# Queries and keys of a hybrid attention layer by Strassen's scheme: a projection stage of its own, operands through DRAM

## The chip, the cores and the metric

The kernel runs on one core of a Trainium2 chip. The metric is the device time of one execution in microseconds, here the median of three runs. TensorE (PE in the profile) multiplies matrices, VectorE (DVE) and ScalarE (ACT) work elementwise, GpSimd (POOL) does some elementwise work and issues DMAs that the other queues cannot, and SyncE (SP) issues most of the DMAs.

## The reference

One decoder layer over a sequence of 1024 tokens of width 1024, in float32:

```python
h = rms_norm(x, pre_mix_g)
qa, ka, va, qb, kb, vb, gates = split(h @ w_in)       # 512 x3, 1536 x3, 2048 columns
qa, ka = rope(qa), rope(ka)                           # 4 heads x 2 parts of 64
oa = diff_attention(qa, ka, va, lam)                  # causal, softmax1 - lam * softmax2
ya = rms_norm(oa) * (1 - lam_init) @ w_a_out
qb, kb = rope(qb), rope(kb)                           # 3 groups x 4 heads of 128
outs, lses = dilated_group(...)                       # windows 128, 512, 2048; dilations 1, 4, 16
yb = (softmax(lses) weighted sum of outs) @ w_b_out
x = x + rms_norm((sigmoid(g_a) * ya + sigmoid(g_b) * yb) @ w_mix_out)
u = causal_depthwise_conv(rms_norm(x) @ w_up)         # 2 x 2816 channels
x = x + rms_norm((gelu(u_gate) * u_val) @ w_down)
```

## The kernel before

Every float32 operand is split into a high and a low part (`split`: ScalarE writes the rounded high part, VectorE the remainder), and every product is three matmuls, high x high, low x high and high x low (`mm3`, L155 to L157). x is held transposed as `xh` and `xl`, the eight chunks of 128 channels side by side; the norm's factor is applied after the product (`rstd_row`, and inside the rope tables).

The program runs in stages. The *value stage* computes the 2048 value columns by Strassen's scheme in Winograd's form: x is cut into quarters (b11, b12, b21, b22), three sums of them (t2, t3, t4) stand beside the quarters, and a fourth (minus t1) stands in b12's own place; seven products of half the depth take the place of eight. Afterwards b12 is loaded again and split (`again`, `split_x`). Values go to DRAM (`v_d`) in POOL's queue, and so do the rope tables (`tab_d`).

Then come *queries, keys, gates and attention*. `proj_t` computes one block of 128 columns: two halves of 512 tokens, eight chunks, 48 matmuls. For a query or key `rotated` applies the rope (L684 to L687: ScalarE swaps the halves, VectorE multiplies and adds), and the high and low parts are written straight into `slot` tiles (18 of them, 512 KB each, used by operands and values alike). For a gate `put_gate` scales the block and stores it to `gt_d`.

Attention is a row of jobs. In attention A (four heads) a job is a block of 128 queries: `attend_a` computes both scores, a masked reduction on VectorE (L770), the exponential on ScalarE (L777), and the two softmaxes' combination (L784). Transposes on TensorE (L697), their split, and the products with the values (L710, L713) are put off by `later` to following jobs. In attention B there are twelve steps (two pairs of heads x three groups x two heads) of four jobs (`attend_b`: scores L155 to L157 into `s`, reduction L975, exponential L981, output L1009). Outputs and their statistics go to DRAM and are merged over the three groups by `merge`, whose loads are in POOL's queue.

`interleave` weaves the pieces of projections between the jobs by weight: in A, the query and key of the next head and the gates named in `A_FILLS` ("g" a gate, "p" the next head, "P" the first step of B, "v", "w", "x", "V" values); in a step of B, the query and key of the next step; in the last step three gates (`B_GATES`). The order of the instructions on each engine comes from a planner that runs the program against a cost model, with priorities where `high_priority` raises them; the chip then runs each engine's list in order. `issue_after` (`behind_marks`) holds some work behind marked instructions.

After attention come the two output projections (`branch`), the mixing product, the up projection with its convolution (the first blocks plain, the other nineteen by the same scheme of seven products, `seven`), the down projection by seven products, and the norms.

Of the kernel before, what the change touches and what calls it, by code (L numbers as in the profile page):

```python
# [15 lines left out]
F32 = mybir.dt.float32  # L16
# [33 lines left out]
START_GATES, A_FILLS, B_GATES = 1, ("gpgg", "gpvgg", "wgpgg", "xgPVgg"), 3  # L50
# [37 lines left out]
def trunk(ctx: ExitStack, tc: tile.TileContext, a, out):  # L88
# [133 lines left out]
    c_d = dram.tile([NF, P, S], F32, name="c_d")  # L222

# [90 lines left out]
    rstd_row = open_pool(attn, "row", side="right").tile([P, S], F32, name="rstd_row")  # L314
    st_a = ExitStack()
# [5 lines left out]
    tb = open_pool(st_v, "tb", side="right")  # L321
# [12 lines left out]

    def new_tabs():
        return [tabs.tile([P, S], F32, tag=t, name=t) for t in ("cos", "sin")]
# [17 lines left out]
    def load_tabs(first, n):  # L354

        cos, sin = new_tabs()
        for q in range(P // n):
            to = slice(q * n, (q + 1) * n)
            dma(cos[to], tab_d[0][first : first + n])
            dma(sin[to], tab_d[1 if q % 2 else 2][first : first + n])  # L360
        return cos, sin

# [11 lines left out]
    def sums_x(k, low, high):  # L374
# [3 lines left out]
        e, o = (tb.tile([P, 2, 512], F32, tag=t, name=t) for t in ("sin", "cos"))  # L378
# [17 lines left out]
    def norm_x(m):  # L396
# [5 lines left out]
        if m < 8:  # L402
            rows_x.append(tb.tile([P, S], F32, tag=("kk", "ang", "sin", "cos")[m % 4], name="rows"))
            nc.gpsimd.dma_start(rows_x[m], a["x"][m * P : (m + 1) * P])
# [40 lines left out]
    with ExitStack() as st_y:  # L445
# [17 lines left out]
        def more_tags():  # L463

            for tag in itertools.cycle(("ang", "kk", "sin", "cos")):
                t = tb.tile([P, S], F32, tag=tag, name="raw")
                for sl in halves():
                    yield t[:, sl]
                    yield next(rt_tags)
# [142 lines left out]
        made, fetched, again = 12, 14, []  # L612
# [3 lines left out]
        for n in range(8, len(steps_v)):  # L616
# [15 lines left out]
            if n == ANGLES_AT:  # L632
                pos = [load_raw(a["positions"][sl].partition_broadcast(P), next(tags)) for sl in halves()]
                args = [tb.tile([P, S], F32, tag=n_, name=n_) for n_ in ("sin", "cos")]
# [20 lines left out]
    tabs = open_pool(attn, "tabs", side="right")  # L655
    cos_a, sin_a = load_tabs(64, 32)
# [21 lines left out]

    def rotated(ps, cos, sin, sl, quarter):
        t1 = rt.tile([P, 512], F32, tag="t1", name="t1")  # L680
        t2 = rt.tile([P, 512], F32, tag="t2", name="t2")
        for q in range(P // quarter):
            src, dst = slice((q ^ 1) * quarter, ((q ^ 1) + 1) * quarter), slice(q * quarter, (q + 1) * quarter)
            nc.scalar.activation(t1[dst], ps[src], AF.Copy)  # L684
        nc.vector.tensor_tensor(t2, ps, cos[:, sl], op=ALU.mult)  # L685
        nc.vector.tensor_tensor(t1, t1, sin[:, sl], op=ALU.mult)
        nc.vector.tensor_tensor(t2, t2, t1, op=ALU.add)  # L687
        return t2
# [37 lines left out]
    def proj_a(h, res):  # L726
        q0, q1, k0, k1, l0, l1 = (slot(n) for n in ("q0", "q1", "k0", "k1", "l0", "l1"))
        res += [q0, q1, k0, k1, l0, l1]

        def put_q(half, sl, ps):  # L730
            t = rotated(ps, cos_a, sin_a, sl, 32)
            nc.scalar.activation(q0[u, sl], t[u], AF.Copy)
            nc.scalar.activation(q1[v, sl], t[v], AF.Copy)
            nc.vector.tensor_tensor(q0[v, sl], t[u], q0[u, sl].bitcast(F32), op=ALU.subtract)
            nc.vector.tensor_tensor(q1[u, sl], t[v], q1[v, sl].bitcast(F32), op=ALU.subtract)

        def put_k(half, sl, ps):
            t = rotated(ps, cos_a, sin_a, sl, 32)
            for part, kk in ((u, k0), (v, k1)):
# [1003 lines left out]
```

## Time and profile before

| | |
|---|---|
| Median of three runs | 1696.95 us (1696.14 to 1698.37) |
| The profiled execution | 1697.3 us, its span 1695.3 us |
| Granted TensorE clock | 0.998 |
| TensorE / VectorE / ScalarE / GpSimd busy | 1682.1 / 1333.5 / 891.8 / 106.3 us |
| DMA | 216.41 MB, 128 GB/s over the span |

A group's row gives source line, engine, operation, tiles and shape, count, then busy us and mean ns of one, then the engine's idle time before such instructions and what ended it. A row of the view by stretches gives the stretch in us from the start, its length, the busy us of PE, PEld (weight loads), DVE, ACT and POOL with the number of instructions, the granted clock, the share of time that the DMA engines were busy, and GB/s. A row of the chain gives start, length, engine, line and count of the work that ended last. In a row of a DMA stand the tile and its source, the queue, the count, the size and the median us to landing. The tile `acc` is the PSUM bank that projections write; `s`, `pt` and `o` are those of attention. Line numbers are those of the kernel before.

### The profile page before, as it was taken

To read this page: it belongs to the slowest core of one execution; us is meant where nothing else is said; L and a number is where in the kernel's file an instruction comes from. 1 tells how busy PE (TensorE), PEld (TensorE's weight loads), DVE (VectorE), ACT (ScalarE), POOL (GpSimd) and SP (SyncE) were. 2 spreads that over 40 slices of the span, in tenths; PEclk is the share of its full clock that TensorE was granted. 3 is DMA by queue.
4 is the path that set the end of the run, shared out by engine and by line. 5 is a ranking of instruction groups with operands and counts; after the bars stand their busy time and mean duration, and the time that the engine had idled before them with its cause. 6 is when DMAs were issued, how large, how long until landed. Compare 5 with 4: busy or idle time off the path is not lost.

```text
span 1695.3 us, 22960 instructions
## 1 busy us (share of the span) xinstructions
PE 1682.1 (99%) x8078; PEld 1410.0 (83%) x8078; DVE 1333.5 (79%) x2445; ACT 891.8 (53%) x1663; POOL 106.3 (6%) x174
## 2 busy tenths in 40 slices
PE   9999999999999999999999999999999999999997
PEld 7888888888888888888888888888888888888886
DVE  8795686877776766677756865899999989799967
ACT  7643575656454776666653533464444445355453
POOL 0031000000000000000123400300000000000000
PEclk9999999999999999999999999999999999999999
DMA  8677311214112213233585631132222222296524
GB/s 266 234 253 235 99 60 62 86 59 119 50 63 81 70 53 108 86 112 119 200 285 186 203 118 63 38 106 92 95 81 75 98 83 88 95 343 214 193 75 161
DMA packets 104451, 216.41 MB, mean 128 GB/s; under 512 B 12992, under 2 KB 22144, under 8 KB 104336
## 3 DMA queue, kind: packets, MB, share of 16 engines
q1 hardware_dynamic: 89296, 171.28, 30.5%
q0 software_dynamic: 10288, 35.28, 6.1%
q10 hardware_dynamic: 4752, 8.39, 1.3%
q8 instruction: 63, 1.03, 0.3%
q14 instruction: 52, 0.43, 0.1%
HBM read 167.05 MB, written 47.86 MB: 127 GB/s over the span
## 4 chain that ended last, share of the span: by engine, by line
PE 97%; DMA 2%; DVE 1%; ACT 1%; issue 0%; SPq 0%; DVEq 0%
PE acc L155 22%; PE acc L156 22%; PE acc L157 22%; PE acc L1578 3%; PE acc L1579 3%; PE acc L1577 3%; PE o L710 2%; PE pt L697 2%; PE acc L1258 2%; PE acc L1256 2%; PE acc L1257 2%; PE o L713 1%; PE s L156 1%; PE s L157 1%; PE s L155 1%; PE s L768 1%
## 5 line engine op out<-in xcount | busy, mean ns | idle before, releaser
L156 PE MATMUL acc<-xh,wlo 128*128 128x512 f32 x768 | 303.2, 395 | 0.0
L157 PE MATMUL acc<-xl,whi 128*128 128x512 f32 x768 | 303.1, 395 | 0.0
L155 PE MATMUL acc<-xh,whi 128*128 128x512 f32 x768 | 303.0, 395 | 0.0
L149 ACT ACTIVATE whi<-raw 128x512 fp32r<-128x512 f32 (+1 forms) x252 | 156.1, 626 | 170.3 <-PE acc L157 88.1
L146 DVE TENSOR_TENSOR wlo<-raw,whi 128x512 fp32r<-128x512 f32 (+1 forms) x252 | 178.8, 717 | 40.4 <-ACT whi L149 34.7
L156 PEld LDWEIGHTS acc<-xh,wlo 128*128 128x128 f32 x768 | 144.4, 188 | 27.8
L157 PEld LDWEIGHTS acc<-xl,whi 128*128 128x128 f32 x768 | 144.5, 188 | 27.5
L155 PEld LDWEIGHTS acc<-xh,whi 128*128 128x128 f32 x768 | 144.4, 188 | 27.3
L155 PE MATMUL acc<-mh,whi 128*128 128x512 f32 x400 | 155.8, 390 | 0.3 <-ACT mh L149 0.3
L156 PE MATMUL acc<-mh,wlo 128*128 128x512 f32 x400 | 155.6, 389 | 0.0
L157 PE MATMUL acc<-ml,whi 128*128 128x512 f32 x400 | 155.3, 389 | 0.0
L684 ACT ACTIVATE t<-acc 64x512 f32<-64x512 f32 (+1 forms) x160 | 94.7, 592 | 55.3 <-PE acc L157 53.3
L1454 DVE TENSOR_TENSOR u<-acc,u 128x512 f32<-128x512 f32 x133 | 91.3, 691 | 20.3 <-PE acc L157 20.1
L149 ACT ACTIVATE whi<-s 128x512 fp32r<-128x512 f32 x76 | 46.9, 627 | 102.3 <-PE acc L157 88.1
L685 DVE TENSOR_TENSOR t<-acc,cos 128x512 f32<-128x512 f32 x64 | 44.1, 690 | 67.1 <-ACT t L684 63.5
L155 PEld LDWEIGHTS acc<-mh,whi 128*128 128x128 f32 x400 | 75.1, 188 | 16.0 <-ACT mh L149 0.5
L156 PEld LDWEIGHTS acc<-mh,wlo 128*128 128x128 f32 x400 | 75.1, 188 | 15.6
L157 PEld LDWEIGHTS acc<-ml,whi 128*128 128x128 f32 x400 | 75.1, 188 | 15.5
L1578 PE MATMUL acc<-whi,wlo 128*128 128x512 f32 x220 | 77.6, 390 | 0.0
L1577 PE MATMUL acc<-whi 128*128 128x512 f32 x220 | 76.4, 389 | 0.0
L1579 PE MATMUL acc<-wlo,whi 128*128 128x512 f32 x220 | 73.2, 390 | 0.0
L777 ACT ACTIVATE s<-s,mx 128x896 f32<-128x896 f32 (+7 forms) x64 | 49.4, 772 | 36.9 <-DVE mx L770 21.0
(387 smaller groups left out, 3941.6 us busy)
## 6 DMA issues: line engine op xcount, KB each, us to landing
raw<-in_w_in SPq DMA_DIRECT2D x96, 256.0 KB, 2.9
raw<-in_w_up SPq DMA_DIRECT2D x88, 256.0 KB, 2.8
raw<-in_w_v SPq DMA_DIRECT2D x71, 256.0 KB, 4.7
raw<-c_d SPq DMA_DIRECT2D x48, 256.0 KB, 3.8
c_d<-c SPq DMA_DIRECT2D x22, 512.0 KB, 2.7
raw<-in_w_down SPq DMA_DIRECT2D x37, 256.0 KB, 4.1
v_d<-yv POOLq DMA_DIRECT2D x32, 256.0 KB, 4.5
gt_d<-gate ACTq DMA_DIRECT2D x32, 256.0 KB, 2.1
```

Source lines behind the costliest of these rows:

```text
L146: eng.tensor_tensor(lo, src, hi.bitcast(F32), op=ALU.subtract)
L149: copy = nc.scalar.activation(hi, src, AF.Copy)
L155: nc.tensor.matmul(o, sh, mh, start=first, stop=False, skip_group_check=on)
L156: nc.tensor.matmul(o, sl, mh, start=False, stop=False, skip_group_check=on)
L157: nc.tensor.matmul(o, sh, ml, start=False, stop=last, skip_group_check=on)
L684: nc.scalar.activation(t1[dst], ps[src], AF.Copy)
L685: nc.vector.tensor_tensor(t2, ps, cos[:, sl], op=ALU.mult)
L777: exp = nc.scalar.activation(sc[c][:, :w], sc[c][:, :w], AF.Exp, bias=mx[:, c, 0:1], scale=-1.0, accum_out=den[:, c : c + 1])
L1454: nc.vector.tensor_tensor(to, made(p), x, op=ALU.add)
L1577: nc.tensor.matmul(banks[m], gh[:, tk], wh, start=f == 0, stop=False)
L1578: nc.tensor.matmul(banks[m], gl[:, tk], wh, start=False, stop=False)
L1579: nc.tensor.matmul(banks[m], gh[:, tk], wl, start=False, stop=f == NH - 1)
```

## The change

A stage of its own, behind the value stage, computes all sixteen query/key pairs by seven products: query and key block of a head are the two halves of the columns, and the quarters and sums of x from the value stage are used once more. The four sums of the weight quarters (s1 to s4) are made in a tile that ScalarE or a load fills first, and to which DMAs of POOL's queue add the rest. ScalarE and VectorE evacuate, rotate and split each pair over 1024 tokens, and four stores put it into `qk_d`, already in the order that the dilation needs. xh is restored after this stage instead of inside the value stage. Attention loads its operands: twelve loads of 256 KB for a head of A, four of 512 KB for a step of B. What is woven between the jobs is now gates alone, in pieces of six matmuls (a gate is eight pieces): one gate at the start, 20, 20, 16 and 16 pieces in the heads of A, four in each of eleven steps of B, and four in the last.

```diff
-START_GATES, A_FILLS, B_GATES = 1, ("gpgg", "gpvgg", "wgpgg", "xgPVgg"), 3
+START_GATES, A_FILLS, B_GATES = 8, ("gpgggg", "gpgvggg", "wgpggg", "xgPgVgg"), 4
...
+    qk_d = dram.tile([2 * (AH + BG * BH), 2, P, S], F32, name="qk_d")
...
-            if (p, i) == ("p5", 1):
-
-                again.append(load_raw(a["xT"][k][:, 512:], next(tags)))
-            if (p, i) == ("p6", 1):
-                with behind_marks():
-                    split_x(k, halves()[1], again[k])
+    with ExitStack() as st_q:
+        pq = open_pool(st_q, "pq")
+        ops_q = dict(p1=("a11", b11), p6=("s2", t2), p2=("a12", b21), p7=("s3", t3), p5=("s1", b12), p4=("a22", t4), p3=("s4", b22))
+        slots_q = itertools.cycle([slot_w, slot_w, lambda: slot_w(pq, 3)])
...
+        def weights_q(n):
...
+            def start_sum(name, src, scale=None):
+                t = pq.tile([P, 512], F32, tag="s", name=name, bufs=4)
+                if scale:
+                    nc.scalar.activation(t, src, AF.Copy, scale=scale)
+                else:
+                    dma(t, src)
+                return t
+
+            def add_to(t, src):
+                nc.gpsimd.dma_start(t, src, accum_op=ALU.add)
+
+            a11 = load_raw(d11, next(tags))
+            s1 = start_sum("s1", d21)
+            put_w("a11", a11)
+            s3 = start_sum("s3", s1, -1.0)
+            add_to(s1, d22)
+            add_to(s3, d11)
+            s2 = start_sum("s2", a11, -1.0)
+            add_to(s2, s1)
+            a12 = load_raw(d12, next(tags))
+            a22 = load_raw(d22, next(tags))
+            put_w("s2", s2)
+            put_w("a12", a12)
+            s4 = start_sum("s4", s2, -1.0)
+            add_to(s4, d12)
+            put_w("s3", s3)
+            put_w("s1", s1)
+            put_w("a22", a22)
+            put_w("s4", s4)
...
+        def rotate_q(n, c, u, tab):
...
+            for q in range(P // quarter):
+                src, dst = slice((q ^ 1) * quarter, ((q ^ 1) + 1) * quarter), slice(q * quarter, (q + 1) * quarter)
+                nc.scalar.activation(sw[dst], u[src], AF.Copy)
+            nc.vector.tensor_tensor(u, u, tab[0], op=ALU.mult)
+            nc.vector.tensor_tensor(sw, sw, tab[1], op=ALU.mult)
+            nc.vector.tensor_tensor(u, u, sw, op=ALU.add)
...
+                split(*(t.rearrange("p (r i) -> p r i", r=dil) for t in (hi, lo)), u.rearrange("p (i r) -> p r i", r=dil))
+            for i, t in enumerate((hi, lo)):
+                dma(qk_d[2 * head + c, i], f32(t))
+
+        def seven_q(n, ws, tab):
...
+            left = next(banks_q)()
+            made("p1", left, True)
+            with tc.high_priority(offset=60):
+                nc.scalar.activation(c11, left, AF.Copy)
+            down = next(banks_q)()
+            made("p6", down, True)
+            plus_q(c12, down, c11)
+            made("p2", left)
+            made("p7", down)
+            plus_q(c22, down, c11)
+            right = next(banks_q)()
+            made("p5", right, True)
+            plus_q(c22, right, c22)
+            made("p4", down)
+            plus_q(c21, down, c11)
+            with tc.high_priority(offset=60):
+                nc.scalar.activation(c11, left, AF.Copy)
+            made("p3", right)
+            plus_q(c12, right, c12)
+            for c, u in enumerate(us):
+                rotate_q(n, c, u, tab)
...
+        for n in range(len(pairs)):
+            following = weights_q(n + 1) if n + 1 < len(pairs) else None
+            if n == AH:
+                tab = load_tabs(0, 64)
+            seven_q(n, ws, tab)
+            ws = following
+        again = [load_raw(a["xT"][k][:, 512:], next(tags)) for k in range(4)]
+        with tc.high_priority(offset=60):
+            for k in range(4):
+                split_x(k, halves()[1], again[k])
...
-    def proj_a(h, res):
+    def load_a(h, res):
...
+        for to, src in ((q0[u], qh[u]), (q0[v], ql[u]), (k0[u], kh[u]), (k0[v], kh[u]), (l0[u], kl[u]), (l0[v], kl[u]),
+                        (q1[v], qh[v]), (q1[u], ql[v]), (k1[u], kh[v]), (k1[v], kh[v]), (l1[u], kl[v]), (l1[v], kl[v])):
+            dma(f32(to), src)
...
-    def proj_b(g, h, res, between=None):
+    def load_b(g, h, res):
+        ops = [slot(n) for n in ("qh", "ql", "kh", "kl")]
+        res += ops
+        at = order.index(QB + g * 512 + h * P)
+        for n, t in enumerate(ops):
+            dma(f32(t), qk_d[at + n // 2, n % 2])
...
-        fill = proj_b(nxt[1], nxt[2], ops_b[nxt], functools.partial(split_b, *nxt[:2]) if h % 2 else None)
-        interleave(jobs(todo), 4, (itertools.chain(fill, once(load_ots)) if nxt == steps[-1] else fill, 8))
+        fills = [(once(functools.partial(load_b, *nxt[1:], ops_b[nxt])), 0), gates(2)]
+        if h % 2:
+            fills.append((once(functools.partial(split_b, *nxt[:2])), 0))
+        fills.append(gates(2))
+        if nxt == steps[-1]:
+            fills.append((once(load_ots), 0))
+        interleave(jobs(todo), 4, *fills)
```

More of the change, by code (lines that the diff above doesn't have):

```diff
@@ L852, in head_norm @@
         later(3, norm)
-    free_gates = list(range(2 * KC))
+    supply = itertools.chain(*(gate(i) for i in range(2 * KC)))
     def gates(n):
-        todo = [free_gates.pop(0) for _ in range(n)]
-        return itertools.chain(*(gate(i) for i in todo)), 4 * n
+        return itertools.islice(supply, n), n * 0.5
     def run(gen):
```

121 lines of the change are left out of this document (56 added, 65 removed).

## The prediction

> **What bounds the kernel now.** I read the page's busy line and chain first, then the busy time by stage, then the chain restricted to one stage, which gives true matmul intervals.
>
> ```profile
> span 1695.3 us, 22960 instructions
> PE 1682.1 (99%) x8078; PEld 1410.0 (83%) x8078; DVE 1333.5 (79%) x2445; ACT 891.8 (53%) x1663; POOL 106.3 (6%) x174
> PE 97%; DMA 2%; DVE 1%; ACT 1%; issue 0%; SPq 0%; DVEq 0%
> ...
> L155 PE MATMUL acc<-xh,whi 128*128 128x512 f32 x768 | 303.0, 395 | 0.0
> ```
> ```profile
> 26.00:162.00 136.00, 136.00 (x603) 112.42 (x604) 111.55 (x196) 69.49 (x120) 23.07 (x40) 1.00 0.71 235
> 162.00:865.00 703.00, 703.00 (x3743) 601.25 (x3742) 497.21 (x1180) 430.68 (x901) 24.67 (x44) 1.00 0.30 97
> 240.00:545.00 305.00, 305.00 (x1616) 261.01 (x1614) 225.27 (x588) 166.04 (x350) 1.14 (x4) 1.00 0.23 76
> 545.00:865.00 320.00, 320.00 (x1781) 275.53 (x1780) 221.06 (x501) 216.43 (x472) 21.06 (x34) 1.00 0.35 117
> 1110.00:1480.00 370.00, 370.00 (x1633) 306.28 (x1632) 338.01 (x452) 161.24 (x222) 3.79 (x39) 1.00 0.26 89
> ```
>
> The second view lists stretch, length, then busy us of PE, PEld, DVE, ACT, POOL, then clock, DMA share, GB/s. Its rows are the value projection (26 to 162), all queries, keys, gates and attention (162 to 865), inside it attention A (240 to 545) and B (545 to 865), and the up projection by Strassen's scheme (1110 to 1480). TensorE has no gap in any of them. The kernel is bound by the number of matmuls, so only that number, or a new gap, can move the time.
>
> The 395 ns of a matmul is not its price: matmuls overlap. 1633 of them in 370 us are 0.2266 us each, and the chain agrees with four in 0.91 us:
>
> ```profile
> 1505.28 0.91 PE acc L1577 x4
> ```
>
> **The change, part by part.**
>
> *Fewer matmuls.* A query/key pair is 2 columns x 2 halves x 8 chunks x 3 = 96 matmuls; with seven products of 4 chunks it is 84. Sixteen pairs save 192 x 0.2266 = 43.5 us. By the 395 ns of the group row it would look like 76 us, which is why I take the interval. The profiled execution took 1697.3 us (span 1695.3 and 2.0 around it; the median of the runs is 1696.95, 0.35 lower), so without a single new gap the kernel would take 1697.3 - 43.5 = 1653.8 us. Everything else is a question of new gaps.
>
> *The query/key stage (16 x 84 x 0.2266 = 19.04 us each pair).* Its costs on the other engines, by these rows:
>
> ```profile
> L146 DVE TENSOR_TENSOR wlo<-raw,whi 128x512 fp32r<-128x512 f32 x40 | 27.5, 688 | 5.4 <-ACT whi L149 5.2
> L1454 DVE TENSOR_TENSOR u<-acc,u 128x512 f32<-128x512 f32 x133 | 91.3, 691 | 20.3 <-PE acc L157 20.1
> L1339 DVE SCALAR_TENSOR_TENSOR c<-u,cw,c 128x1024 f32<-128x1024 f32 x44 | 55.2, 1284 | 3.9 <-ACT c L1338 3.4
> L1343 DVE TENSOR_TENSOR c<-c 128x1024 f32<-128x1024 f32 x22 | 26.9, 1224 | 0.1
> 572.52 2.12 DVE L878 TENSOR_TENSOR kl<-t,kh 128x512 fp32r<-128x512 f32 x2 [0.33 <-ACT kh L877]
> L149 ACT ACTIVATE whi<-raw 128x512 fp32r<-128x512 f32 x40 | 25.2, 629 | 17.2 <-PE acc L157 16.7
> L684 ACT ACTIVATE t<-acc 32x512 f32<-32x512 f32 x32 | 18.9, 590 | 7.6 <-PE acc L157 7.2
> L149 ACT ACTIVATE vh<-vperm 128x1024 fp32r<-128x1024 f32 x16 | 16.5, 1048 | 0.1
> ```
>
> DVE: 7 weight remainders and 5 additions to PSUM at 0.69, 6 wide rotations and 2 remainders at 1.22, together 18.1 us. In the 8 pairs with a dilation of 4 or 8 the remainders read strided, 2.12 each, and it is 19.9. The up projection is my scale: there a block also has 84 matmuls, and 17 operations at 0.69, 4 at 1.28 and one at 1.22 sum to 18.1, while the row shows 338/370 x 19.04 = 17.4 busy and no gap. By that ratio the strided pairs need 19.1, as much as TensorE. ACT: 7 splits and 3 scaled copies at 0.63, 2 copies from PSUM at 0.59, 2 splits at 1.05, and 8 part copies in an attention A pair (the A row shows that 32 partitions cost what 64 do; over 1024 columns 1.05), 18.1 us; in a B pair only 4 such copies. Every evacuation has one product, 12 x 0.2266 = 2.72 us, before TensorE needs its bank again, and one strided remainder can stand in front of it. I take 0.5 us in each of 8 strided pairs: +4 us (0 to 16, all sixteen at 1 us).
>
> *The accumulating DMAs* are not in this trace. Nearest rows:
>
> ```profile
> raw<-in_w_in SPq DMA_DIRECT2D x96, 256.0 KB, 2.9
> v_d<-yv POOLq DMA_DIRECT2D x32, 256.0 KB, 4.5
> og<-og_d POOLq DMA_DIRECT2D x8, 768.0 KB, 6.4
> ```
>
> Each is 256 KB from POOL's queue: 4.5 us if it is a plain transfer, 9 if reading and writing the target doubles it. A set of weights has three in series (s1, s2, s4) behind one load: 2.9 + 3 x 4.5 + copies, about 19 us, or 32. Weights are issued a pair ahead, and nine operand slots serve seven products, so up to 1.7 pairs (32 us) cover it; I take nothing. Uncovered, ACT's copy s4 = -s2 stands in its queue waiting for the DMA, the copies of c11 behind it, and product p2 behind those: that is the second rival. Bytes are no bound here: 8 x 0.26 + 4 x 0.52 = 4.2 MB per 19.04 us is 220 GB/s, below the 235 of the value stage. Against a gain: POOL's queue is otherwise empty then.
>
> *Into and out of the stage.* The first pair's sums wait for buffers of the value stage while its stores run on POOL: +1 us. The restore of xh (four 256 KB loads, four splits) moves from the value stage, past the last pair's stores in SP's queue; the first gate's second half needs it 5.4 us into START_GATES; +2 (0 to 6).
>
> *Attention A.* Four heads lose 8 units of projection and get 80 pieces of gates in all (a piece is 6 matmuls, 1.36 us), 20 or 16 a head. From the chain:
>
> ```profile
> by line: PE acc L156 24.0%; PE acc L155 23.9%; PE acc L157 23.9%; PE o L710 6.0%; PE s L768 5.1%; PE pt L697 5.1%; PE s L767 5.0%; PE o L713 3.4%; PE o L839 2.1%; PE pt L847 1.1%; PE s L155 0.2%; PE s L156 0.2%; PE s L157 0.2%
> L156 PE MATMUL acc<-xh,wlo 128*128 128x512 f32 x343 | 136.2, 397 | 0.0
> L155 PE MATMUL acc<-xh,whi 128*128 128x512 f32 x342 | 135.8, 397 | 0.0
> L157 PE MATMUL acc<-xl,whi 128*128 128x512 f32 x342 | 135.8, 397 | 0.0
> ```
>
> The first row (240 to 540) gives 28% of 300 us to attention, some 21 us a head. With 27 or 22 us of gates a head falls from 76 to 49 or 44 us. DVE had 225 us in 305, 56 a head. At 0.69 an operation it loses 40 (24 of rotating and splitting a q and a k column, 4 of their weights, 12 of three gates; 27.6 us) and gets 10 for 2.5 gates (6.9): 35 of 49 us. It does not become the bound, but there is less to run while the softmax goes round: +3 (0 to 10).
>
> ```profile
> POOL mask_b L938 <- DMA oa_d<-osb: 353.8, 1, 353.8
> ```
>
> B's first reduction needs mask_b, and POOL makes it only behind A's last store. The end of A (weight 12 of the last head's 64) has 3 pieces, 4 us, of gates beside it instead of 10: +2 (0 to 6).
>
> *Attention B.* The last three rows are of 545 to 865: 1027 projection matmuls, 232.7 us, leave 87.3 for attention. With 48 pieces (65.3 us) the stage needs 152.6 us of TensorE, 12.7 a step instead of 26.7. ACT had 216 us; the rows below take 44.5, 21.1, 19.0 and 23.9 from it, and 12 splits for gates put 7.5 back: 115, no bound. DVE (221) loses as much. The transfers are the new thing:
>
> ```profile
> L684 ACT ACTIVATE t<-acc 64x512 f32<-64x512 f32 x75 | 44.5, 593 | 22.7 <-PE acc L157 21.7
> L877 ACT ACTIVATE kh<-t 128x512 fp32r<-128x512 f32 x20 | 21.1, 1058 | 14.9 <-DVE t L687 14.9
> L877 ACT ACTIVATE qh<-t 128x512 fp32r<-128x512 f32 x18 | 19.0, 1057 | 10.5 <-DVE t L687 10.5
> L149 ACT ACTIVATE whi<-raw 128x512 fp32r<-128x512 f32 x38 | 23.9, 628 | 2.8 <-PE acc L157 2.3
> ```
> ```profile
> DMA packets 18410, 37.40 MB, mean 117 GB/s; under 512 B 2941, under 2 KB 7197, under 8 KB 18385
> raw<-in_w_in SPq DMA_DIRECT2D x36, 256.0 KB, 2.8
> gt_d<-gate ACTq DMA_DIRECT2D x5, 256.0 KB, 3.8
> GB/s 266 234 253 235 99 60 62 86 59 119 50 63 81 70 53 108 86 112 119 200 285 186 203 118 63 38 106 92 95 81 75 98 83 88 95 343 214 193 75 161
> 860.00:870.00 10.00, 10.00 (x51) 8.45 (x50) 3.26 (x6) 5.47 (x7) 0.53 (x1) 1.00 1.00 394
> ```
>
> Of the 37.4 MB of 545 to 865, 24 weight loads go (-6.3), 7 gate stores come (+1.8), and 11 loads of four 512 KB operands come (+23.1): 56 MB in 152.6 us, 367 GB/s. The best 10 us of the trace moved 394, the best slice (42 us) 343, the value stage 235 on average. At 394 the bytes take 142 us and hide; at 343, 163 (+11); at 235, 238 (+86). They are long rows, like those of the best slice, so I take 343, and 3 more for steps whose operands land late: +14. A step's slots come free when the scores of the step before are done, so a load cannot start earlier. The Trainium skill, "DMA: Bandwidth & Descriptors", section Bandwidth, gives about 358 GB/s for a core's share of HBM; by it the bytes take 156 us and this term is +4 before late landings instead of +11. The 394 of the trace is above that figure.
>
> *The tail.* The last step has 4 pieces of gates instead of 24, with the splits of oa and the merge of head 2 in it; branch A follows 27 us earlier against the same DMA chain: +3 (0 to 10).
>
> Sum: 1653.8 + 4 + 1 + 2 + 3 + 2 + 14 + 3 = 1682.8; I say 1682.
>
> **The rivals.**
>
> *All of it hides* (gaps under 14 us): 1654 to 1668. For it: DVE at 91% made no gap in the up projection, and gates can be moved ahead of the step that owns them. Against: attention has never run here with so little beside it. 25%.
>
> *The sums come late (slower).* Place: the query/key stage, ACT waiting in order for an accumulating DMA. If each takes over 9 us, the chain passes 32 us and the pair follows it: at 11 us each the chain is 2.9 + 33 + 2 = 38 us in 1.7 pairs, 22.3 a pair, +3.3 x 16 = 52, and with the other terms (25) 1731. It decides from 1.2 us a pair, (43.5 - 25) / 16. For it: the price is unseen. Against: slots for nearly two pairs. 12%.
>
> *B follows its transfers* at 270 GB/s or less: 56 MB in 207 us, +54; with the other 15, 1723. For it: the merges' loads all fall in steps 7 to 11. Against: the rate of the best slice. 13%.
>
> *The clock drops in the gaps.* The end of the trace shows it, clock in the eighth column:
>
> ```profile
> 1680.00:1685.00 5.00, 5.00 (x24) 4.14 (x23) 4.96 (x14) 0.93 (x3) 0.00 (x0) 1.00 0.91 296
> 1685.00:1690.00 5.00, 0.48 (x3) 0.06 (x1) 4.17 (x13) 1.13 (x4) 0.00 (x0) 0.97 0.86 297
> 1690.00:1695.00 5.00, 0.00 (x0) 0.00 (x0) 1.42 (x2) 0.00 (x0) 0.00 (x0) 0.50 0.42 158
> ```
>
> Some 4 us after the last matmul the clock is 0.50. If eleven steps of B each waited over 4 us and then ran some us at half speed, it would be 11 x 6 = 66 us over 1653.8, about 1720. "TensorE: Matmul & The Clock Gate" in the Trainium skill, Part 1, gives the same: a gap of about 3.4 us halves the clock. 3%.
>
> **How the numbers follow.** The forecast, part of the gain given back in B, has 47% and a range of its own of 1668 to 1699. A measurement tells 0.2%, 3.4 us, from no change. Faster (below 1693.5): the 25 and 38 of the 47; same: 9; slower: 28 with the three slow rivals. The range, 1656 to 1722, leaves out some 6 in 100 below, of the rival in which all hides, and 14 above, the far half of the slow ones.
>
> **What would show it.** Right: 7886 matmuls; the query/key stage 16 pairs at 19.0 to 19.5 us with DVE at 90% or more; in B PE idle at scores that wait for qh or kh loads, GB/s above 300. Wrong: gaps whose releaser is s1, s2 or s4; a clock below 1.00 in B; or gaps in A behind the softmax rows.

## The result, and the profile after

The changed kernel takes 1838.22 us (median of four runs, 1833.92 to 1838.64) against 1696.65 for the kernel before in the same comparison (1696.14 to 1698.37): 1.083 times as long, 95% interval 1.081 to 1.085. The forecast was 1682, its range ended at 1722. The change makes the kernel slower by 141.6 us; the experiments below take it apart as far as they reach.

The page of the changed kernel, parts 1, 4 and 6:

```profile
span 1836.8 us, 23152 instructions
PE 1716.3 (93%) x7886; PEld 1415.8 (77%) x7886; DVE 1382.7 (75%) x2413; ACT 922.3 (50%) x1647; POOL 166.6 (9%) x238
PE 66%; DMA 14%; issue 7%; DVE 7%; ACT 6%; POOL 0%; SPq 0%; DVEq 0%; POOLq 0%; ACTq 0%
...
s<-in_w_in POOLq DMA_DIRECT2D x48, 256.0 KB, 5.0
s<-s POOLq DMA_DIRECT2D x16, 256.0 KB, 3.8
```

The matmuls went as foreseen, 8078 to 7886. But where TensorE held 97% of the chain it holds 66%, and DMAs have 14%. The view by stretches tells where (the columns are those of the prediction: PE, PEld, DVE, ACT and POOL busy, then clock, DMA share, GB/s):

```profile
26.00:161.00 135.00, 135.00 (x601) 111.80 (x600) 105.53 (x187) 63.64 (x111) 25.59 (x40) 1.00 0.72 237
161.00:550.00 389.00, 340.03 (x1389) 269.40 (x1388) 272.64 (x321) 238.20 (x309) 57.73 (x68) 0.94 0.64 172
550.00:842.00 292.00, 272.22 (x1411) 228.51 (x1410) 190.96 (x535) 122.18 (x270) 4.80 (x8) 0.96 0.52 161
842.00:979.00 137.00, 112.86 (x707) 99.62 (x706) 70.74 (x265) 91.97 (x283) 10.41 (x16) 0.81 0.72 257
979.00:1018.00 39.00, 28.98 (x141) 23.76 (x140) 25.02 (x54) 19.42 (x39) 11.79 (x19) 0.91 0.77 265
1018.00:1093.00 75.00, 71.14 (x298) 57.92 (x298) 56.37 (x79) 35.36 (x52) 28.62 (x33) 0.96 0.60 205
1093.00:1196.00 103.00, 103.00 (x484) 85.81 (x483) 67.05 (x132) 38.77 (x94) 6.51 (x5) 1.00 0.33 118
```

The rows are the value stage, the query/key stage, attention A, B, the two branches, and the mixing product. The value stage and all from 1093 on are as before. Between them lie 932 us, where the kernel before had 791 (162 to 953), all filled. Less the 43.5 us of the matmuls removed that is 747, so 185 us are gaps and slow clock. The last evacuation of the query/key stage begins at 549.4: 388 us, of which the 1344 matmuls of the products are 304.6 and 45 other matmuls 10, so some 74 us are lost there. The other 111 lie in attention and the branches.

What holds the stage stands in its waits (161 to 550: who waited <- for what: us in total, times, longest) and in the chain of 160 to 300 (start, us, what):

```profile
POOL s L675 <- ACT s L669: 237.3, 35, 11.6
ACT whi L149 <- DMA s<-in_w_in: 42.7, 12, 6.9
ACT whi L149 <- DMA s<-s: 31.7, 9, 9.2
PE acc L155 <- ACT whi L149: 16.9, 6, 7.8
```
```profile
by line: DMA s<-in_w_in 33.3%; issue 29.1%; DMA s<-s 17.3%; ACT sw L704 3.0%; ACT s L669 2.5%; ACT whi L149 2.2%; ACT qkh L149 2.1%; DVE u L707 1.7%; DVE wlo L146 1.6%; DVE qkl L146 1.5%; DVE sw L706 1.1%; DVE u L729 1.0%; POOL s L675 1.0%;
...
220.39 5.36 DMA s<-s
229.30 4.48 DMA s<-in_w_in
240.23 8.04 DMA s<-in_w_in
250.93 4.30 DMA s<-in_w_in
```

TensorE waits for a split (`whi`), the split for an accumulating DMA, the DMA's issue on POOL for a negated copy on ScalarE (L669). No matmul's line is among the largest shares of this chain: the sums set the pace. Another 29.1% of it is "issue", time for which the profile shows no wait.

### The profile page after: what moved, and what is told of

Read it like the earlier page. It is cut to its first block, busy times and chain, and to the rows that moved or that the text cites. A ratio compares the mean times of both kernels' runs of the same rounds, so it can differ in the third digit from the quotient of the medians.

```text
span 1836.8 us, 23152 instructions
## 1 busy us (share of the span) xinstructions
PE 1716.3 (93%) x7886; PEld 1415.8 (77%) x7886; DVE 1382.7 (75%) x2413; ACT 922.3 (50%) x1647; POOL 166.6 (9%) x238
## 4 chain that ended last, share of the span: by engine, by line
PE 66%; DMA 14%; issue 7%; DVE 7%; ACT 6%; POOL 0%; SPq 0%; DVEq 0%; POOLq 0%; ACTq 0%
PE acc L155 12%; PE acc L156 12%; PE acc L157 12%; DMA s<-in_w_in 5%; PE acc L1662 3%; PE acc L1661 3%; PE acc L1660 3%; DMA s<-s 2%; PE o L818 2%; DMA mw<-e_d 2%; PE acc L1339 2%; PE acc L1341 2%; PE acc L1340 2%; PE pt L805 1%; PE s L155 1%
## 5 line engine op out<-in xcount | busy, mean ns | idle before, releaser
L155 PE MATMUL acc<-xh,whi 128*128 128x512 f32 x352 | 139.9, 399 | 12.9 <-ACT u L734 10.1
L146 DVE TENSOR_TENSOR wlo<-s,whi 128x512 fp32r<-128x512 f32 x140 | 95.3, 687 | 67.1 <-ACT whi L149 66.8
L156 PE MATMUL acc<-xh,wlo 128*128 128x512 f32 x352 | 140.2, 399 | 0.8 <-DVE wlo L146 0.8
L157 PE MATMUL acc<-xl,whi 128*128 128x512 f32 x352 | 139.6, 397 | 0.0
L818 PE MATMUL o<-pt,vh 128*128 128x256 f32 (+1 forms) x376 | 78.2, 316 | 24.0 <-ACT osb L1087 21.9
L818 PEld LDWEIGHTS o<-pt,vh 128*128 128x128 f32 x376 | 64.5, 220 | 35.4 <-ACT osb L1087 29.2
L155 PEld LDWEIGHTS acc<-xh,whi 128*128 128x128 f32 x352 | 67.3, 191 | 28.2 <-ACT u L734 11.3
L704 ACT ACTIVATE sw<-u 64x1024 f32<-64x1024 f32 (+1 forms) x80 | 84.7, 1059 | 2.1 <-DVE u L729 0.8
L156 PEld LDWEIGHTS acc<-xh,wlo 128*128 128x128 f32 x352 | 67.6, 192 | 14.6 <-DVE wlo L146 1.3
L157 PEld LDWEIGHTS acc<-xl,whi 128*128 128x128 f32 x352 | 67.5, 192 | 13.6
```

The lines of the kernel that those rows point to most:

```text
L146: eng.tensor_tensor(lo, src, hi.bitcast(F32), op=ALU.subtract)
L155: nc.tensor.matmul(o, sh, mh, start=first, stop=False, skip_group_check=on)
L156: nc.tensor.matmul(o, sl, mh, start=False, stop=False, skip_group_check=on)
L157: nc.tensor.matmul(o, sh, ml, start=False, stop=last, skip_group_check=on)
L704: nc.scalar.activation(sw[dst], u[src], AF.Copy)
L818: nc.tensor.matmul(o[:, q0 : q1 + 1], vs[b // 4][0][:, b % 4, c], t[:, part], start=first and n == part == 0, stop=False)
```

## The experiments

Each was run once, beside the kernel before (1696.8 to 1698.6), so a few us tell nothing. "Stage" is the query/key stage, 161 to its last evacuation; 388 us in the changed kernel.

**The sums left out.** `s1 = load(d21)`, `s2 = load(d22)`, and so on: no negated copies, no accumulating DMA.

> Left out: the additions in the weight sums; s1 to s4 are each one plain 256 KB load of a block, with no copy on ScalarE and no DMA that adds. Theory 'late sums' (the chain of copies and adding DMAs starves TensorE in the query/key stage, 389 us from the end of the value stage to the last evacuation for 305 us of its matmuls): the stage falls to 305-320 us and the program from 1838 to 1755-1775 us. Rival 'own load' (evacuation, rotation and splits on ScalarE and VectorE bound the stage): the stage stays above 365 us, the program above 1810.

1772.06 us, stage 322. The row of mid-stage, first of the changed kernel, then of this one:

```profile
200.00:460.00 260.00, 224.40 (x915) 177.15 (x914) 185.27 (x216) 165.57 (x214) 39.30 (x45) 0.94 0.65 175
```
```profile
161.00:200.00 39.00, 38.31 (x169) 31.38 (x168) 20.44 (x29) 22.12 (x33) 1.67 (x4) 1.00 0.46 142
200.00:460.00 260.00, 259.07 (x1141) 213.47 (x1140) 232.51 (x272) 180.17 (x216) 0.00 (x0) 1.00 0.59 205
```

84 matmuls in 19.1 us against 23.9: without sums the middle of the stage has no gap, evacuations, rotations, strided splits and stores included. The sums cost 66 us, and 118 us over the 1653.8 of a kernel without gaps remain elsewhere.

**The sums by GpSimd**, from plain loads:

```diff
-            s1 = start_sum("s1", d21); ...; add_to(s1, d22)
+            s1 = combined(nc.gpsimd, "s1", a21, a22, ALU.add)   # s2, s3, s4 alike
```

> The four sums are made complete, by four elementwise operations on GpSimd from plain loads, in place of copies and adding DMAs. Late sums: a chain of three 1.5 us operations in place of three DMAs and their copies; the stage falls to 310-330 us, the program to 1765-1790. Own load: above 365 and above 1810, as the splits and rotations are the same.

1799.17 us, stage 345: of the stage's 66 us, 43 come back. A likely reason why not all do stands in VectorE's groups in the stage (170 to 480), first the changed kernel's, then this one's:

```profile
L146 DVE TENSOR_TENSOR wlo<-s,whi 128x512 fp32r<-128x512 f32 x56 | 38.1, 689 | 61.1 <-ACT whi L149 61.1
```
```profile
L146 DVE TENSOR_TENSOR wlo<-s,whi 128x512 fp32r<-128x512 f32 x63 | 57.6, 920 | 6.8 <-ACT whi L149 6.6
L730 DVE TENSOR_TENSOR u<-acc,u 128x512 f32<-128x512 f32 x30 | 20.3, 679 | 3.0 <-PE acc L157 3.0
```

The same subtraction takes 920 ns beside GpSimd's additions instead of 689, while additions that take one input from a PSUM bank (`u<-acc,u`) stay at 679. VectorE is busy 311 us of 345, and of the 15 us that TensorE stands idle in the stage its waits put 12 down to VectorE. The Trainium skill, "SBUF — State Buffer", section "SBUF: two separate sides", has VectorE instructions with two inputs in SBUF share a port with GpSimd's reads; these rows agree.

**The gates held at their steps.** All matmuls of a gate wait for the last scores traced:

```diff
+                with tc.issue_after(scored[-1]) if scored else nullcontext():
                     mm3(ps, wh[:, w], wl[:, w], ...)
```

> Nothing left out; every six matmuls of a gate are queued on TensorE behind the last scores written before them, so the planner can't run gates ahead of the attention step that owns them. Theory 'gates spent early' (all sixteen gates had run by 778 us, before attention B began at 842): from 842 on, B and the branches take 252 us for 174 us of matmuls; this falls by 40-60 us beyond the moved gates, the program to 1775-1800, and the clock in B is 0.95 or more. Rival 'transfers' (B waits for the loads of its operands): gates move, but the program stays within 12 us of 1838.

1825.92 us, just outside the 12 us of the rival, whose reason (loads of operands) is tested below. The observation behind the theory is this row of the changed kernel, all 32 evacuations of gates:

```profile
L251 DVE TENSOR_TENSOR gate<-acc,rstd_row x32: 678/691/699, 546.1 to 777.8; 128x512 f32<-128x512 f32 x32
```

They end at 777.8, B begins at 843: the planner had run the forty-eight pieces meant for B long before it. Held back, they bring only 12 us. That the gates were spent early is true; undoing it brings back a small part of the loss.

**Both**, GpSimd sums and held gates:

> Both edits: sums on GpSimd and gates queued behind scores. If the two causes are separate, their gains add: 1705-1745 us. If one hides the other, the gain is that of the larger one: 1765-1790.

1781.79 us, 17 better than the sums alone: the two gains of 39 and 12 us add, to 56. Attention and branches now take 530 us (506 to 1036). Of their 443 us of matmuls the first gate's 11 run inside the stage, so 98 us are lost although the rest of the fill is where the forecast put it. The first of it is this idle stretch behind the stage, below it the longest wait and two rows of SyncE's queue:

```profile
506.00:530.00 24.00, 0.99 (x2) 0.50 (x2) 11.99 (x10) 8.73 (x7) 1.94 (x3) 0.50 0.71 225
```
```profile
PE s L864 <- DMA k<-qk_d: 30.2, 2, 26.5
```
```profile
518.93 1.97 SPq L718 DMA_DIRECT2D qk_d<-qkl  x2
521.08 1.66 SPq L844 DMA_DIRECT2D q<-qk_d  x2
```

The operands that TensorE waits for are those of the first pair, which went to `qk_d` between 205.8 and 217. Their loads are issued right behind the last pair's stores.

**The first operands' loads from ScalarE's queue** in that kernel: `load_a(0, ops[0], nc.scalar.dma_start)`.

> The kernel with GpSimd sums and pinned gates (1781.8), and the twelve loads of attention A's first operands issued from ScalarE's queue instead of SyncE's. Theory 'SyncE's queue': the hole of 26.5 us at the start of attention A is the wait of these loads behind the last pair's stores. Then the hole falls to 8 to 14 us and the time to 1764 to 1772. Rival 'the loads cannot start earlier': their buffers lie where the last pair's operands were. Then the hole and the time stay (1778 to 1785).

1782.58 us, and the hole stays: in ScalarE's queue, too, the loads stood behind a split of the last pair (it begins at 515.17, the first load is issued at 516.46). That does not tell whether the buffers would have allowed more; where the hole comes from is open between order and memory.

**More gates ahead of A** in the same kernel, 24 pieces for 8:

> The kernel with GpSimd sums and pinned gates (1781.8), with 24 instead of 8 pieces of gates ahead of attention A (32.6 us of matmuls instead of 10.9) and 16 pieces fewer inside A. Theory 'a hole at A's start': TensorE stands idle for 26.5 us there, since the first operands pass through the rotation, the store and the load after the last product; the 16 pieces fill 21.8 us of it, and A gives back 6 to 12 us for what it loses of its fill. Time 1764 to 1776. Rival 'A needs every piece more': A grows by as much as the hole shrinks; 1778 to 1786.

1773.30 us, in the expected range: A with its hole falls from 252 to 241 us, and B and the branches give some 3 back. The expectation's words on the hole are not right: by the rows above, it is not the first operands that pass through rotation and store there, but the last pair's.

**Half the operand loads of B**: `res += [qh, qh, kh, kh]`, two loads a step instead of four.

> Attention B loads only the high halves of its queries and keys (two of four operands a step; the high half is used in place of the low one, so the low part of the scores is left out). Nothing else changes, matmuls included. Theory 'B follows its transfers': B moved some 35 MB in 137 us (257 GB/s), 11.5 MB go, and at that rate B and the time fall by 40 to 45 us, to 1793 to 1800. Rival 'B follows the softmax chain': a step's scores, reduction, exponentials, transposes and value products in series set some 12 us a step when no other matmuls lie between them. Then B stays within 5 us and the time at 1832 to 1840.

1837.78 us. B from first to last reduction, changed kernel and this one:

```profile
843.00:988.00 145.00, 119.12 (x744) 105.19 (x744) 78.98 (x296) 97.45 (x298) 13.67 (x21) 0.82 0.71 252
```
```profile
846.00:986.00 140.00, 119.63 (x757) 106.89 (x758) 77.88 (x283) 97.50 (x299) 12.01 (x18) 0.84 0.58 193
```

252 GB/s become 193, and B stays within 5 us and the time within 1: B does not follow its transfers.

**B's outputs into the three accumulator banks** instead of one bank: `po = psum()` for `psum(F32, ps_o, "o")`.

> The changed kernel; attention B's value products go to the three accumulator banks, which stand idle in B once the gates are done, instead of the one bank of their own. Theory 'B runs on its own round': a step without other matmuls is set by the hand-over between TensorE, ScalarE and VectorE, above all by the one bank that ScalarE must empty (15 to 22 us of waits in 137). Then B falls by 12 to 30 us (the clock recovers too), and the time to 1810 to 1826. Rival 'the round is in the scores, exponentials and transposes': the waits move there, B stays within 6 us and the time at 1832 to 1840.

1820.43 us, in the expected range, but not cleanly. TensorE's largest waits in B, changed kernel (843 to 988) and this one (804 to 963):

```profile
PE o L818 <- ACT osb L1087: 15.4, 19, 4.3
PE s L155 <- DVE stat L1053: 3.9, 7, 1.3
```
```profile
PE acc L155 <- ACT osb L1087: 4.9, 4, 2.8
PE s L155 <- DVE stat L1053: 2.2, 2, 1.3
```

The wait for the one bank is gone; but gates and outputs now take turns in the same banks, so gates stayed in B as well (their last at 970.6). The 18 us are the two effects together.

**All gates ahead of attention**, on GpSimd sums: `START_GATES = 128`. This measures attention with nothing beside it.

> The kernel with GpSimd sums, and all sixteen gates (768 matmuls, 174 us) run in one stretch after the query/key stage, so that attention A and B have nothing beside them: this measures both bare. Theory 'attention needs fill': A's matmuls are some 84 us and B's 87; bare, B takes the 145 us that it takes in the changed kernel, and A 150 to 190 us instead of 84, so the whole comes to 1830 to 1870 against 1799. Rival 'the loss lies in the hole at A's start and in the tail': A bare takes under 120 us, the hole is covered by the gates, and the whole is 1780 to 1800 or less.

1834.24 us. Bare attention A, then bare B:

```profile
662.00:831.00 169.00, 127.08 (x681) 104.90 (x679) 133.14 (x458) 90.23 (x230) 1.24 (x4) 0.81 0.35 103
831.00:993.00 162.00, 134.72 (x763) 121.31 (x764) 83.75 (x292) 100.38 (x301) 15.80 (x25) 0.74 0.70 248
```

The prediction had 84 us of matmuls in A and 87 in B. Bare they take 169 and 162, with no engine busy over 83%. That points to the round through TensorE, VectorE, ScalarE and back. Some 160 us are lost when no other matmuls fill it, and not all of them are idle time: at granted clocks of 0.81 and 0.74 the clock costs up to 0.19 x 169 + 0.26 x 162 = 74 us of them, by this estimate.

**Five pairs only by the scheme**, steps 2, 4, 6, 8 and 10 of B, GpSimd sums; A and the other steps project directly as before, one column beside each step of B:

```diff
+    pairs = [pairs[n] for n in (2, 4, 6, 8, 10)]
...
+        fills = [(proj_b(*steps[m][1:], ops_b[steps[m]], c), 4) for m, c in COLUMNS[n]]
```

> Strassen's scheme for five of the sixteen pairs only (the operands of steps 2, 4, 6, 8 and 10 of attention B), with GpSimd sums. All of attention A and the other steps of B project directly as in the kernel before; a direct pair is split so that each step of B has one column (48 matmuls, 10.9 us) beside it; gates as before. 60 matmuls fewer, 13.6 us. Theory 'the gaps are missing fill': steps with 10.9 us of projection beside 7.3 us of attention are longer than the some 12 to 15 us of the softmax chain and keep their gaps under 1 us; the query/key stage loses 2.5 us a pair as with GpSimd sums in all sixteen, 12 us. Time 1693 to 1704. Rival 'whatever goes through DRAM costs': each loaded operand or the stage's start and end cost by themselves; then 1710 to 1725.

1710.59 us, 7 above the range and at the lower edge of the rival's. B, first to last reduction, and below it a part of the branches:

```profile
645.00:864.00 219.00, 212.99 (x1287) 186.31 (x1286) 149.39 (x397) 151.86 (x373) 15.19 (x24) 1.00 0.49 166
900.00:940.00 40.00, 34.86 (x137) 27.57 (x136) 23.62 (x32) 9.85 (x16) 9.46 (x16) 0.91 0.67 217
```

B holds 558 matmuls of projections and gates (126 us) beside attention's 87, and takes 219, with TensorE idle for 6 and no load of operands among its larger waits. With no fill a step is 12.0 us (the 145 us above), 4.7 of them lost; with 5.4 us of gates (held gates and GpSimd sums, 178 us in B) 14.8, 2.1 lost; with 10.9 us some 0.5. But 40 us of branches hold 137 matmuls (179 where they are full, below): the chain of merges behind B's last outputs (store 8.51, load 6.47, three loads of weights at 6.2 to 6.8 in the chain) is not covered any more.

**16 pieces of gates moved from A to B's last step** in that kernel:

> The kernel with five pairs by Strassen's scheme (1710.6), with 16 pieces of gates (21.8 us) moved from the first and the last head of attention A to the last step of B. Theory 'the tail needs fill': the branches behind B lose some 11 us there, since the chain of merges (store, load, weights, products) ends later than a shorter B lets TensorE reach it; the pieces cover 8 to 11 of it and A gives back 0 to 4: 1700 to 1707. Rival 'A needs its pieces more': 1709 to 1716.

1713.98 us, in the rival's range. The branches are full, and A has the gaps:

```profile
480.00:500.00 20.00, 16.89 (x76) 13.30 (x75) 19.55 (x46) 12.79 (x23) 0.00 (x0) 0.91 0.50 132
640.00:660.00 20.00, 14.96 (x105) 14.20 (x105) 13.59 (x51) 13.13 (x40) 0.00 (x0) 0.83 0.04 14
900.00:940.00 40.00, 40.00 (x179) 33.10 (x178) 26.60 (x47) 11.58 (x18) 7.71 (x15) 1.00 0.62 207
```

What covers the tail is missing in A: the fill is limited, and moving it only moves the gap.

**What holds the sums.** Five kernels kept all the accumulating DMAs and changed what stands around them. The negated copies on GpSimd (`nc.gpsimd.tensor_scalar(t, src, -1.0, ...)`):

> The three negated copies with which the sums begin (s2, s3, s4) are made by GpSimd instead of ScalarE; everything else is the changed kernel. Theory 'ScalarE waits in order': the transfers are quick enough (5.0 and 3.8 us each), and what stretches the query/key stage from some 312 to 389 us is that a copy waiting for a transfer holds every later split and evacuation in ScalarE's queue. Then the stage falls to 330 to 350 us and the time from 1838 to 1780 to 1800. Rival 'the chain itself is too long': load, three transfers in series and their copies take longer than a pair (19 us) plus what the buffers allow, whoever makes the copies. Then the stage stays at 375 us or more and the time at 1825 to 1840.

Eight buffers for the sums (`bufs=8`, `qkh` and `qkl` with one):

> The changed kernel with eight buffers for the weight sums instead of four (one instead of two for each rotated half makes the room). With four, each pair's s1 to s4 go into the buffers of the pair before, so a pair's first load must wait until the sum that stood there has been split, which in turn waits for an operand slot. Theory 'four buffers undo the cover': with eight the chain of the next pair starts some 10 us earlier and its transfers run beside the products; the query/key stage falls from 388 us to 320 to 345 and the time to 1772 to 1795. Rival 'GpSimd's queue or the transfers in series set the pace': the stage stays at 375 to 395 us, the time at 1825 to 1845.

Both together:

> The changed kernel with both: the negated copies by GpSimd, and eight buffers for the sums. Each alone left the stage at 386 and 392 us. Theory 'each held what the other freed': with the copies on ScalarE, the next pair's first copies stand in its queue behind the split of this pair's s4; with four buffers, the next pair's first load stands behind the split that empties the buffer; either way the next chain (some 20 us from the first copies to s4) begins only when this one has ended, and a pair takes 23 to 24 us. With both gone the chains of two pairs overlap, and GpSimd itself needs some 15 us a pair: stage 320 to 345 us, time 1770 to 1800. Rival 'the transfers in series set the pace whatever starts them': stage 375 us or more, time 1825 to 1840.

The links a pair apart in program order (eight buffers; copies on ScalarE):

```diff
+        for n in range(len(pairs)):
+            second_sum(n + 1)      # s2 += s1
+            first_sums(n + 2)      # s3 = -s1; s2 = -s2; s1 += d22; s3 += d11
+            six_q(n + 1, following)
             seven_q(n, ws, tab)
+            last_sum(n + 1, following)   # s4 = -s2; s4 += d12
+            load_sums(n + 3)
```

> The same sums by the same accumulating DMAs and copies on ScalarE, but their links put a pair apart in program order: s1 and the base of s2 are loaded nearly three pairs ahead, s1 and s3 are completed two pairs ahead, s2 one, s4 half a pair (eight buffers; one load of 256 KB more a pair). No copy and no transfer then follows in its queue straight behind the transfer that it needs. Theory 'an engine waits in order for each link': a pair's links sum to some 20 us or more of waiting in whichever queue holds them, and no choice of engine or of buffers alone removes that, only distance; the stage falls from 388 us to 315 to 340, the time to 1762 to 1790. Rival 'the accumulating transfers themselves (64 of 256 KB, read and written) are the limit': the stage stays at 370 us or more, the time at 1820 to 1840.

The same with the copies on GpSimd:

> The staggered sums, with their three negated copies on GpSimd instead of ScalarE. With the copies on ScalarE a pair took 21.1 us in mid-stage (1035 matmuls in the 260 us from 200 to 460, against 915 in the changed kernel and 1141 without additions), and the copies still stand there behind the 4.3 to 8.6 us of the rotation's copies and behind splits that wait for a sum. Theory 'an engine waits in order for each link': with distance and with copies on a queue of their own the links are off every other engine's way; mid-stage 19.1 to 20 us a pair (1090 to 1141 matmuls), stage 335 to 355 us with the late start, time 1785 to 1803. Rival 'the transfers are the limit': mid-stage stays at 21 us or more, stage 368 us or more, time 1815 to 1825.

| kernel | time | stage | matmuls 161 to 200 | 200 to 460 |
|---|---|---|---|---|
| changed kernel | 1838.2 | 388 | 113 | 915 |
| copies on GpSimd | 1834.6 | 387 | 93 | 979 |
| eight buffers | 1838.8 | 393 | 107 | 944 |
| both | 1835.8 | 384 | 86 | 1011 |
| links a pair apart | 1819.7 | 372 | 88 | 1035 |
| apart, copies on GpSimd | 1808.1 | 361 | 119 | 1031 |
| sums by GpSimd | 1799.2 | 345 | 151 | 1067 |
| no sums | 1772.1 | 322 | 169 | 1141 |

"Stage" in us; the last two columns count matmuls between these times. Three of my theories fell in turn: ScalarE's order alone, the buffers alone, both together bring 4 us or less. (With both, a pair in mid-stage falls from 23.9 to 21.6 us, but the first pairs and the last lose it again.) Only distance between the links brought more, 18 us, and 30 with the copies moved as well, where 33 to 73 of the stage were expected. Mid-stage it gives 21.1 us a pair; the 19.1 without sums was never reached. The first of these two kernels met the stage bound of the rival "the transfers are the limit" (372 us, against 370), the second lay between the forecasts. So waits in order explain at most half of the 66 us, and the rest is open. The row of the kernel with links apart and copies on GpSimd shows DMA engines busier than without sums (0.79 against 0.59) for nearly the same GB/s:

```profile
200.00:460.00 260.00, 246.07 (x1031) 196.79 (x1030) 213.57 (x245) 163.79 (x201) 113.34 (x93) 0.97 0.79 217
```

Why they are busier stands in the queues of the changed kernel in the same stretch (packets, MB, share of the 16 engines' time; q1 is the plain transfers of SyncE's queue, q0 the accumulating ones of GpSimd's) and, last, in q0 of the value stage before (26 to 162), where it holds plain transfers:

```profile
q1 hardware_dynamic: 12388, 33.53, 36.8%
q0 software_dynamic: 6435, 11.71, 27.7%
...
q0 software_dynamic: 3824, 13.11, 26.8%
```

Per MB the accumulating transfers hold the 16 engines for 0.277 x 260 / 11.71 = 6.2 us, plain ones of either queue for 2.9 (q1) and 2.8 (0.268 x 136 / 13.11): twice as long. Whether this is what takes the rest is not shown. The waits of the kernel with links apart and copies on GpSimd speak rather against it: between 200 and 460 TensorE is idle for 14 us, put down to VectorE's additions and ScalarE's splits and copies, and ScalarE's splits wait for a transfer only 5.9 us:

```profile
PE s L155 <- DVE u L742: 4.5, 2, 3.2
ACT whi L149 <- DMA s<-in_w_in: 5.9, 4, 3.8
```

**The repairs together**: links apart, held gates, 24 pieces ahead of A.

> All that helped, together: staggered sums, gates pinned to their steps, 24 pieces of gates ahead of attention A. With GpSimd sums in place of staggered ones the same kernel took 1773.3 (stage 345 us). Theory 'an engine waits in order for each link': the stage takes 315 to 340 us and the time is 1743 to 1770. Rival 'the transfers are the limit': stage 370 us or more, 1798 or more. Either way attention keeps some 75 us of gaps: still slower than the kernel before.

1792.94 us, stage 372. Here the rival's bound for the stage held and the time lay between the two. The best version with all sixteen pairs stays the one with GpSimd sums (1773.3), 76 us behind the kernel before; the one with five pairs is 12 behind. None beats it.

## Why the prediction was wrong, point by point

*Fewer matmuls, and no other price*: right on the matmuls. 192 went, and the stages that the change does not touch kept their times.

*The stage's evacuations, +4*: right in kind, and without sums not even that: 19.1 us a pair.

*The accumulating DMAs, "I take nothing"*: the first step that failed. Their times came near the lower bound (5.0 and 3.8 us as medians of the whole run, 4.8 and 5.2 between 200 and 460, against bounds of 4.5 and 9), for which the chain of three was "about 19 us". The cover of "1.7 pairs (32 us)" was not there. It counted operand slots alone. With the same slots the stage has no gap without sums, and with more buffers, another queue for the copies and more distance 30 us came back; what takes the rest is open. The rival "the sums come late" named the place and the wait (ScalarE behind a transfer, products behind it), but made it depend on transfers of over 9 us. The chain of 19 us, the quick case, took 4.8 us a pair, more than the 3.3 that the rival gave for its slow one. Measured: 66 us, and by the table 56 matmuls (12.7 us) of it in the first 39 us of the stage, where the first pair's chain has nothing before it. The *+1* for the first pair was this term, too small by a factor of ten.

*Out of the stage, +2*: the step looked at xh and its split and not at the loads of A's first operands. These come behind the last pair's rotation and stores, although the operands themselves had been stored some 300 us earlier: 26.5 us of an idle TensorE with the gates held. In the changed kernel gates ran there instead, and were missing later.

*Attention A, +3*: the second failed step. I compared sums of busy time ("35 of 49 us" on VectorE), and no engine became the bound indeed; what was missing is the time of the round. Bare A takes 169 us for 84 of matmuls. With 20 and 16 pieces a head, as planned, A took 252 us, its hole included, 67 more than the 185 of its matmuls (84, and 444 of gates at 0.2266).

*mask_b, +2*: B's first reduction comes 8 us behind A's last output (835.5 to 843.3). Nothing was tested on it alone.

*Attention B, +14 for its transfers*: the sum had the wrong mechanism. Halving the operand loads moved nothing. B took 12.0 us a step, with none of the 48 pieces of gates beside it that the step counted on. The first rival's "gates can be moved ahead of the step that owns them" stood there as a help; the planner did just this, and B had none left.

*The tail, +3*: right in direction and place; measured on the kernel of five pairs, 42 matmuls or 9.5 us. In the changed kernel TensorE is idle for 14 of the branches' 114 us.

*The clock*: right that it drops. The rival asked for a wait of over 4 us in each of eleven steps; the longest wait in B is 4.3 us, most are far shorter, and B's clock was 0.81 all the same. Two places 2 us apart in B show what it means (start, us, operation):

```profile
906.13 0.41 PE L156 MATMUL s<-kh,ql 128*128 128x256 f32 x1
906.34 0.41 PE L157 MATMUL s<-kl,qh 128*128 128x256 f32 x1
906.56 0.41 PE L155 MATMUL s<-kh,qh 128*128 128x256 f32 x1
...
908.74 0.28 PE L157 MATMUL s<-kl,qh 128*128 128x256 f32 x1
908.86 0.28 PE L155 MATMUL s<-kh,qh 128*128 128x256 f32 x1
908.98 0.28 PE L156 MATMUL s<-kh,ql 128*128 128x256 f32 x1
```

The same matmul follows the last one after 0.21 us, then after 0.12. The Trainium skill, "TensorE: Matmul & The Clock Gate", Part 1, has a clock of half speed after idle time; these rows agree on the half, about. They do not show the idle time: the slow stretch begins near 902, and TensorE's only waits in the four us ahead of it are 1.30 and 0.73 us. In the row of B (842 to 979) TensorE is idle for 24 us of 137, and a clock of 0.81 costs at most 0.19 x 137 = 26 more, so the two are of like size, by this estimate.

All three signs of "Wrong" appeared: waits for s1 to s4, a clock below 1.00 in B, and gaps in A. Summed up, of 185 us lost, sums are 66 (left out, they are gone), misplaced gates 12 to 17, the hole at A's start some 9 net. The rest, 93 to 98, lies in attention and the branches. The bare run and the three fills of B's steps show that attention loses time with too little beside it; how the rest divides between gaps, clock and tail is an estimate at best, and no single wait explains it.

## What to carry to other kernels

Matmuls that stand between the links of a latency-bound chain are its cover: moving them to a stage of their own removes the cover with them, so measure the chain with nothing beside it (here 331 us for 171 of matmuls) before taking its fill away; sums of busy times do not show it. A chain of dependent DMAs and copies is not hidden because buffers for it are free: here a chain of some 19 us beside pairs of 19 cost 4.8 us each, and its first round stood open. And a planner that may move filler early will spend it there; see in the trace where it lies, not in the source.

## What the runs showed of the hardware

An accumulating DMA of 256 KB took 5.0 us (from DRAM) or 3.8 (within SBUF), 4.8 and 5.2 in mid-stage, little different from a plain one of that queue (4.5 in the kernel before). But it held the DMA engines about twice as long per MB (6.2 us against 2.8 and 2.9). Beside GpSimd's additions over SBUF, VectorE's subtractions with both inputs in SBUF took 0.92 us instead of 0.69. With accumulating DMAs the DMA engines were busy 0.79 of the time at 217 GB/s, against 0.59 at 205 without.
